# Input-projection tiles as eleven Strassen pairs in a stage of their own, with the gates of two heads beside the seventh pair

## The chip, the cores and the metric

The kernel runs on one core of one Trainium2 chip. The core has five engines with an instruction queue each: TensorE (PE, matrix products, with weight loads that overlap), VectorE (DVE), ScalarE (ACT), GpSimd (POOL) and SyncE (SP, which here only issues transfers). POOL issues transfers as well, and some of these add to what stands in their destination. The metric is the device time of one execution, in microseconds (us).

## The reference, cut to what matters

The kernel computes one decoder block for 512 tokens of width 1024, all in float32. The stage at issue is the first one, the normalised input times one wide weight matrix, and the gated linear attention (GLA) that uses a part of it:

```python
h = rms_norm(x, norm_mix_pre)                       # (512, 1024)
proj = h @ w_in                                     # split by columns:
g_q, g_k, g_v, g_r, g_a, n_q, n_kc, n_vc, n_ks, n_vs, n_kw, n_vw, n_gate, merge_gla, merge_nsa = split(proj)
# gla_mixer, 4 heads, keys of 128, values of 256, chunks of 64 tokens
log_a = log_sigmoid(g_a @ w_alpha2 + b_alpha) / 16
b = cumsum(log_a within a chunk)
qe, ke, kd = q * exp(b), k * exp(-b), k * exp(b_last - b)
o = causal(qe @ ke.T) @ v + qe @ state              # state: decayed sum of kd.T @ v over the chunks before
o = rms_norm(o, per head) * silu(g_r)
```

Behind it come a second attention (compressed, selected and window branches), a merge of the two, an output projection and a SwiGLU feed-forward network (FFN) of width 2816.

## The kernel before, in words

**Number format.** A float32 product is made of three matmuls: each operand is split into a high part (a cast by ACT, L70 or L211) and a low part, the difference to it (DVE, L76 or L212; or ACT writes the negated high part and a POOL transfer adds the raw values from memory to it, L74 and L1102). PE then adds high x high, high x low and low x high in one PSUM bank (`prod`, L194 to L196; the token stage, L274 to L276).

**Stages.** x arrives transposed in eight blocks of 128 features. *Token stage*: the columns whose result is wanted with tokens on the partitions (GLA values, the values of the other attention, its gates and the 16 columns of the low-rank gate) are made in three groups of 440 columns. *Feature-major tiles*: all other columns are made in tiles of 128 output features by 512 tokens, each 24 matmuls of 512 columns: per head a key tile (`gk`) and a query tile (`gq`), eight tiles `r` for the output gate, four query tiles and two key tiles for the other attention (`qst`, `kst`), four merge-gate tiles (`MA`). The weights of one tile (512 KB) are loaded by SP, one tile ahead, and split by the class `Stream`.

**GLA.** Each head has five steps: `gla_prep` (a scan of the log gates, exponentials on ACT, products with q and k on DVE and POOL), `gla_attn` (scores, mask, transposes of `ku`), `gla_state` (the state before each chunk pair), `gla_out` (output, its squares, the mean and its power on POOL, scaling on ACT) and `gla_end` (transposes, product with the output gate, split into `gla_hi` and `gla_lo`). Two more steps, `gates_low` and `gates_gla`, make the log gates of all four heads at once. `weave` spreads the steps of the heads over the tiles: while ACT, DVE and POOL work on a step, PE runs 24-matmul tiles. So the order of work on each engine is written out by the program; the engines take their queues strictly in order, and wait on semaphores.

**A form that exists already.** The FFN runs its gate and up projections as Strassen (Winograd) units: two tiles whose weights and input are cut into halves, seven products instead of eight (L1203), each 4 quarters x 3 = 12 matmuls of 256 columns, 84 for two tiles. Sums of the weights are made by DVE (L1133 to L1140) and split (L1118, L1125); the raw halves get their low part by an accumulating transfer (L1098 to L1102); DVE adds the products together (L1207) on top of a copy by ACT (L1220).

## Time and profile before

| | us |
|---|---|
| Time, median of 3 runs | 862.14 (861.67 to 862.71) |
| Profiled execution, its own time | 862.83 |
| Its span (first to last instruction) | 861.0 |
| PE busy | 846.4 (98%) |
| DVE busy | 596.1 (69%) |
| ACT busy | 485.9 (56%) |
| POOL busy | 142.9 (17%) |
| PE busy from 67 to 241 us (tiles with the GLA) | 173.9 of 174.0 |

In the groups of instructions a row reads: line, engine, operation, output <- input with shapes, count | busy us, mean ns of one | idle time of the engine just before, and what ended it. In a timeline and in the chain of waits the first number is the start in us from the span's start, the second its length; "x84" says that so many instructions stand in the row, and brackets give the idle time before it with its releaser. The chain of waits is the work that ended last, followed back from the end. Neighbouring matmuls overlap in the pipeline, so their price is the distance of their starts.

### The profile page before, as it was taken

How to read it: one execution, taken by the hardware profiler on the slowest of the kernel's cores; microseconds unless marked ns; L12 is line 12 of the kernel's file. 1: busy time of each engine (PE TensorE's matmuls, PEld its weight loads, DVE VectorE, ACT ScalarE, POOL GpSimd, SP SyncE). 2: the span in 40 equal slices, each digit the busy share in tenths (PEclk: the TensorE clock that was granted, in tenths of full speed). 3: DMA queues.
4: the chain of work that ended last, by engine and by line, in shares of the span. 5: the costliest groups of instructions: out<-in, count | busy, mean ns of one | idle time of the engine just before them, and what ended most of it. 6: DMA issues, size and time to landing. Idle time of an engine off the chain costs nothing.

```text
span 861.0 us, 13716 instructions
## 1 busy us (share of the span) xinstructions
PE 846.4 (98%) x5232; PEld 752.4 (87%) x5232; DVE 596.1 (69%) x1099; ACT 485.9 (56%) x866; POOL 142.9 (17%) x169
## 2 busy tenths in 40 slices
PE   8999999999999999999999999999999999999995
PEld 8998888888788788888887999899999999889995
DVE  7224763544466888887666478997778779829876
ACT  6335534333363888887634587666666557535441
POOL 1000322020030100010000265111211110001343
PEclk9999999999999999999999999999999999999998
DMA  6332222312241454445227759679787773325322
GB/s 230 107 95 99 81 93 70 90 57 79 93 144 61 102 120 120 102 106 115 64 84 260 231 152 246 130 181 234 172 180 196 193 164 77 96 89 172 87 99 99
DMA packets 37058, 111.23 MB, mean 129 GB/s; under 512 B 4252, under 2 KB 6572, under 8 KB 36864
## 3 DMA queue, kind: packets, MB, share of 16 engines
...
q14 instruction: 25, 0.20, 0.1%
...
## 4 chain that ended last, share of the span: by engine, by line
PE 91%; ACT 4%; DVE 2%; issue 1%; DMA 1%; POOL 0%; SPq 0%; ACTq 0%; POOLq 0%; DVEq 0%
PE ps_mm L194 11%; PE ps_mm L196 11%; PE ps_mm L195 11%; PE ps_mm L1203 6%; PE ps_tp L1203 6%; PE ps_sc L1203 6%; PE ps_acc L1203 5%; PE ps_sc L1494 4%; PE ps_acc L1494 2%; PE ps_mm L1494 2%; PE ps_tp L804 2%; PE ps_acc L194 1%; PE ps_acc L196 1%; PE ps_acc L195 1%; PE ps_sc L195 1%; PE ps_sc L194 1%
## 5 line engine op out<-in xcount | busy, mean ns | idle before, releaser
L70 ACT CAST whi<-wraw 128x1024 fp32r<-128x1024 f32 (+2 forms) x80 | 79.1, 989 | 149.9 <-PE ps_mm L195 69.5
L194 PE MATMUL ps_mm<-hT_hi,whi 128*128 128x512 f32 x344 | 139.7, 406 | 0.0
L196 PE MATMUL ps_mm<-hT_hi,wlo 128*128 128x512 f32 x344 | 136.8, 398 | 0.0
L195 PE MATMUL ps_mm<-hT_lo,whi 128*128 128x512 f32 x344 | 135.9, 395 | 0.0
L76 DVE TENSOR_TENSOR wlo<-wraw,whi 128x1024 fp32r<-128x1024 f32 (+2 forms) x65 | 74.9, 1152 | 50.9 <-ACT whi L70 50.9
L196 PEld LDWEIGHTS ps_mm<-hT_hi,wlo 128*128 128x128 f32 x344 | 64.6, 188 | 15.5 <-DVE wlo L76 0.3
L194 PEld LDWEIGHTS ps_mm<-hT_hi,whi 128*128 128x128 f32 x344 | 64.7, 188 | 14.1
L195 PEld LDWEIGHTS ps_mm<-hT_lo,whi 128*128 128x128 f32 x344 | 64.8, 188 | 13.1
L764 ACT ACTIVATE p<-p,mx 128x512 f32<-128x512 f32 (+1 forms) x64 | 35.9, 561 | 8.8 <-DVE mx L762 8.2
L212 DVE TENSOR_TENSOR pl<-ps_tp,ph 128x512 fp32r<-128x512 f32 (+1 forms) x64 | 31.0, 489 | 13.2 <-ACT ph L211 12.6
...
L762 DVE CUSTOM_DVE_ANT_0 p<-ps_sc,causal 128x512 f32<-128x512 f32 (+1 forms) x64 | 30.2, 486 | 6.1 <-PE ps_sc L755 6.0
L1102 POOL DMA_DIRECT2D w_uu<-in_w_up x19 | 16.4, 865 | 84.7 <-PE ps_sc L1203 27.1
L211 ACT CAST ph<-ps_tp 128x512 fp32r<-128x512 f32 (+1 forms) x64 | 26.4, 415 | 4.1 <-PE ps_tp L804 3.6
L804 PE MATMUL ps_tp<-ident,p 128*128 128x128 f32 x160 | 27.7, 273 | 0.4 <-ACT pc L698 0.3
L804 PEld LDWEIGHTS ps_tp<-ident,p 128*128 128x128 f32 x160 | 20.6, 140 | 8.0 <-ACT pc L698 0.7
L194 PE MATMUL ps_mm<-gla_hi,whi 128*128 128x512 f32 x64 | 26.2, 409 | 0.0
L196 PE MATMUL ps_mm<-gla_hi,wlo 128*128 128x512 f32 x64 | 25.2, 394 | 0.0
L195 PE MATMUL ps_mm<-gla_lo,whi 128*128 128x512 f32 x64 | 25.2, 394 | 0.0
L479 DVE TENSOR_TENSOR sr<-ps_mm,rb_x 128x512 f32<-128x512 f32 x8 | 5.5, 692 | 27.5 <-PE ps_mm L196 27.5
L1118 ACT CAST w_hl<-s 128x1024 fp32r<-128x1024 f32 x12 | 12.6, 1048 | 19.6 <-issue 15.8
L1118 ACT CAST w_d1h<-s 128x1024 fp32r<-128x1024 f32 x13 | 13.7, 1051 | 17.3 <-issue 12.6
...
## 6 DMA issues: line engine op xcount, KB each, us to landing
wraw<-in_w_t SPq DMA_DIRECT2D x40, 512.0 KB, 3.5
wraw<-in_w_gate SPq DMA_DIRECT2D x21, 512.0 KB, 5.7
rw<-in_w_up SPq DMA_DIRECT2D x19, 512.0 KB, 4.2
wlo<-wraw POOLq DMA_DIRECT2D x15, 512.0 KB, 4.6
wlo<-in_w_gate POOLq DMA_DIRECT2D x13, 512.0 KB, 6.9
w_uu<-in_w_up POOLq DMA_DIRECT2D x19, 256.0 KB, 5.8
...
wraw<-in_w_proj SPq DMA_DIRECT2D x8, 512.0 KB, 3.5
```

The source lines that it names most:

```text
L70: self.nc.scalar.copy(hi[:, :cols], raw[:, :cols])
L76: self.nc.vector.tensor_tensor(out=lo[:, :cols], in0=raw[:, :cols], in1=hi[:, :cols].bitcast(F32), op=OP.subtract)
L194: pe.matmul(ps[:, t], wh[:, c], xh(k)[:, t], start=(k == 0), stop=False)
L195: pe.matmul(ps[:, t], wh[:, c], xl(k)[:, t], start=False, stop=False)
L196: marks.append(pe.matmul(ps[:, t], wl[:, c], xh(k)[:, t], start=False, stop=(k == ktot - 1)))
L211: act.copy(hi, src)
L212: dve.tensor_tensor(out=lo, in0=src, in1=hi.bitcast(F32), op=OP.subtract)
L762: dve.tensor_tensor_reduce(out=o, in0=s, in1=causal[:, S - n:S], scale=-1.0, scalar=-NEG, op0=OP.add, op1=OP.min, accum_out=mx[:, i:i + 1])
L764: act.activation(out=o, in_=o, func=AF.Exp, scale=-1.0, bias=mx[:, i:i + 1], accum_out=z[:, i:i + 1])
L804: pe.transpose(tp[:, i * 128:(i + 1) * 128], p[:, OFF[i] + k * 128:OFF[i] + (k + 1) * 128], ident)
L1203: pe.matmul(o, w[:, c], x[q], start=(first and q == 0 and i == 0), stop=(q == 3 and i == 2), skip_group_check=True)
L1494: pe.matmul(o, w[:, c], x[q], start=(first and q == 0 and i == 0), stop=(q == KH - 1 and i == 2), skip_group_check=True)
```

## The change

22 of the feature-major tiles (four `gk` and `gq` pairs, eight `r`, `kst` s and w, four `qst`) leave the weave and become eleven Strassen pairs, run one after another in a stage of their own (`in_unit`; pairs are counted from 0 to 10). Each pair asks for 84 matmuls of 256 columns on PE, four sums and two lows on DVE, two sum casts and four raw-form instructions on ACT, and two accumulating transfers of 512 and 256 KB on POOL's queue. The input's sums (`t1` to `t4`) are made once, while the second token group runs. Of the three token groups the middle one ("B", the values of heads 1 to 3) moves behind the pairs. The log gates are made for two heads at a time: heads 0 and 1 inside the stage of the pairs, in the queues after pair 6 (the seventh), heads 2 and 3 in the GLA stage. The output gate is one `Silu` in place of `Tanh` and a product. In `gla_prep` two products move from POOL to DVE. The four heads are now woven with the 16 steps of token group B (six matmuls of 440 columns each) and the four `MA` tiles in 32 pieces of three matmuls, in the places that the table `when` gives. ACT loads its tables eight times up to the end of the GLA stage, where it was three times. The stages behind are as before.

Two places show the new order. The first is DVE's queue at the gates. Before (`lam` holds the log gates; `gk_588` and `gq_584` are tiles, `wlo` the low part of a weight tile):

```order
33 L364 TENSOR_SCALAR low<-ps_sc,vecs 128x512 x4
34 L310 TENSOR_TENSOR gk_588<-ps_mm,rb_x 128x512
35 L76 TENSOR_TENSOR wlo<-wraw,whi 128x1024
36 L370 TENSOR_TENSOR lam<-low,lam 128x512 x4
37 L376 SCALAR_TENSOR_TENSOR lam<-keep,lam 128x512
38 L312 SCALAR_TENSOR_TENSOR gq_584<-ps_mm,rb_x 128x512
39 L76 TENSOR_TENSOR wlo<-wraw,whi 128x1024
```

Now, beside pair 7 (L381 are the additions of products, `ps_tp` the banks of pair 7, `ps_sc` of pair 8; L336 to L339 the sums of weights, L206 a low part):

```order
153 L337 TENSOR_TENSOR ssum_165<-ssum_165,wraw 128x512
154 L206 TENSOR_TENSOR s1l<-ssum_166,s1h 128x1024
155 L433 TENSOR_TENSOR lam_1288<-ge_1293,lam_1288 128x512
156 L433 TENSOR_TENSOR lam_1288<-ge_1294,lam_1288 128x512
157 L434 SCALAR_TENSOR_TENSOR lam_1288<-ge_1290,lam_1288 128x512 x2
158 L381 TENSOR_TENSOR r_145<-ps_tp,us_493 128x256
159 L381 TENSOR_TENSOR r_144<-ps_tp,us_493 128x256
160 L402 TENSOR_TENSOR r_145<-r_145,rb_x 128x512
161 L381 TENSOR_TENSOR us_492<-ps_sc,us_492 128x256
```

The scans (L434) were between evacuations of plain tiles; now both stand directly ahead of two additions that empty banks which PE writes again within the same pair.

The second place is PE's queue at the first head's scores. Before:

```order
478 L194 MATMUL ps_mm<-hT_hi,whi 128x512
479 L195 MATMUL ps_mm<-hT_lo,whi 128x512
480 L196 MATMUL ps_mm<-hT_hi,wlo 128x512
481 L420 MATMUL ps_tp<-gq_888,gkx 128x128 x4
482 L427 MATMUL ps_tp<-ident,gku 128x128 x3
483 L194 MATMUL ps_mm<-hT_hi,whi 128x512
```

Now, in the GLA stage (L287 to L289 are the matmuls of token group B, of which 21 stand between the last product of pair 10 and the scores):

```order
1100 L289 MATMUL ps_acc<-wlo,hT_hi 128x440
1101 L287 MATMUL ps_acc<-whi,hT_hi 128x440
1102 L288 MATMUL ps_acc<-whi,hT_lo 128x440
1103 L289 MATMUL ps_acc<-wlo,hT_hi 128x440
1104 L594 MATMUL ps_tp<-gq_1806,gkx 128x128 x4
1105 L601 MATMUL ps_tp<-ident,gku 128x128 x3
1106 L287 MATMUL ps_acc<-whi,hT_hi 128x440
```

What the scores wait for (`gq`, `gkx`, `gku`) comes from `gla_prep(0)`. That step stood among plain tiles; now it begins on ACT after the last copy of pair 10, and the scores stand 21 matmuls behind that pair.

The diff, cut to its core:

```diff
-    with_gla = []
-    for h in range(HG):
-        with_gla += [("h", T_GK + h), ("h", T_GQ + h)]
...
+    for c in range(4):
+        st.plan(("B", c), I["w_tok"][1, :, c * 2 * TG:(c + 1) * 2 * TG], 2 * TG)
+    with_gla = [("h", T_MA + n) for n in range(4)]
...
+    pairs = [(T_GK + h, T_GQ + h) for h in range(HG)] + [(T_R + n, T_R + n + 1) for n in (0, 2, 4, 6)]
+    pairs += [(T_KV + 2, T_KV + 3), (T_NQ, T_NQ + 1), (T_NQ + 2, T_NQ + 3)]
+    NP = len(pairs)
...
+    def in_load(j):
+        g = wts.tile([128, 1024], F32, tag="wraw", bufs=3, name="wraw")
+        nc.sync.dma_start(g, I["w_t"][pairs[j][0]])
+        nc.sync.dma_start(urw[j % 2], I["w_t"][pairs[j][1]])
+        graw[j], uraw[j] = g, urw[j % 2]
+
+    def minus_high(hi, lo, raw, src):
+        act.copy(hi, raw)
+        act.activation(out=lo, in_=raw, func=AF.Copy, scale=-1.0)
+        return pool.dma_start(lo, src, accum_op=OP.add)
+
+    def in_raw_forms(j):
+        hi, lo = slot_of(j, "a")
+        minus_high(hi, lo, graw[j], I["w_t"][pairs[j][0]])
+        wf[j, "a11"], wf[j, "a12"] = [(hi[:, c], lo[:, c]) for c in (slice(0, 512), slice(512, 1024))]
+        t = uu[j % 2]
+        hi, lo = t[:, 0:512], t[:, 512:1024]
+        queued["pool"] = minus_high(hi, lo, uraw[j][:, 512:1024], I["w_t"][pairs[j][1], :, 512:1024])
+        wf[j, "a22"] = (hi, lo)
+
+    def in_sums(j):
+        g, u, (a, b) = graw[j], uraw[j], ssum
+        lo, hi = slice(0, 512), slice(512, 1024)
+        dve.tensor_tensor(out=a[:, lo], in0=u[:, lo], in1=u[:, hi], op=OP.add)
+        dve.tensor_tensor(out=a[:, hi], in0=a[:, lo], in1=g[:, lo], op=OP.subtract)
+        dve.tensor_tensor(out=b[:, lo], in0=g[:, lo], in1=u[:, lo], op=OP.subtract)
+        dve.tensor_tensor(out=b[:, hi], in0=g[:, hi], in1=a[:, hi], op=OP.subtract)
+
+    def slot_of(j, what):
+        n = 3 * j + (1 if what == "a" else 0 if what == "s1" else 2)
+        return slots[n % 5]
...
+    def in_unit(j):
+        tag = ("sc", "mm", "acc", "tp")[j % 4]
+        d1, d2 = [in_dst(n) for n in pairs[j]]
+        p1, p2 = bank(tag), bank(tag)
+        r1, rb, r2, ra = p1[:, 0:256], p1[:, 256:512], p2[:, 0:256], p2[:, 256:512]
+        us = us2[j % 2]
+
+        def product(o, a, b, first):
+            wh, wl = wf.pop((j, a))
+            for q in range(4):
+                c = slice(q * 128, (q + 1) * 128)
+                for i, (w, low) in enumerate(((wh, False), (wh, True), (wl, False))):
+                    pe.matmul(o, w[:, c], x_of(b, q, low), start=(first and q == 0 and i == 0),
+                              stop=(q == 3 and i == 2), skip_group_check=True)
+
+        def add(out, ps, b):
+            return dve.tensor_tensor(out=out, in0=ps, in1=b, op=OP.add)
+
+        product(r1, "a11", "b11", True)
+        act.copy(us[:, 0, :], r1)
+        product(r2, "s2", "t2", True)
+        add(us[:, 0, :], r2, us[:, 0, :])
+        product(rb, "s3", "t3", False)
+        add(us[:, 1, :], rb, us[:, 0, :])
+        product(ra, "s1", "t1", False)
+        add(d2[:, h1], ra, us[:, 1, :])
+        product(rb, "a22", "t4", False)
+        add(d2[:, h0], rb, us[:, 0, :])
+        product(ra, "s4", "b22", False)
+        add(d1[:, h1], ra, us[:, 0, :])
+        product(r1, "a12", "b21", False)
+        act.copy(d1[:, h0], r1)
+        for n, t in zip(pairs[j], (d1, d2)):
+            if T_NQ <= n < T_KV or n < T_GK:
+                queued["dve"] = dve.scalar_tensor_tensor(out=t, in0=t, scalar=0.125 if n >= T_NQ else QSCALE, in1=rb_x,
+                                                         op0=OP.mult, op1=OP.mult)
+            else:
+                queued["dve"] = dve.tensor_tensor(out=t, in0=t, in1=rb_x, op=OP.mult)
+            if n >= T_R:
+                act.activation(out=t, in_=t, func=AF.Silu)
+    def gate_logs(hs, lam, room, tag_low, tag):
+        w_a2, keep, aT, w3, *lows = room
+        pool.dma_start(w_a2, I["w_alpha2"])
+        pool.memset(keep, 1.0)
+        pool.memset(keep[:, :, 0:1], 0.0)
+        dve.memset(aT.bitcast(F32), 0.0)
+        dve.memset(w3.bitcast(F32), 0.0)
+        dve.tensor_copy(w3[0:16, :], w_a2)
+        dve.tensor_copy(w3[64:80, :], w_a2)
+        dve.tensor_tensor(out=w3[32:48, :], in0=w_a2, in1=w3[0:16, :].bitcast(F32), op=OP.subtract)
+        ps = bank(tag_low)
+        for i in range(NT):
+            pe.transpose(ps[0:16, i * 128:(i + 1) * 128], tokb[:, i, C_A:C_A + 16], ident)
+        act.copy(aT[0:16, :], ps[0:16, :])
+        act.copy(aT[32:48, :], ps[0:16, :])
+        dve.tensor_tensor(out=aT[64:80, :], in0=ps[0:16, :], in1=aT[0:16, :].bitcast(F32), op=OP.subtract)
+        for i, h in enumerate(hs):
+            ps = bank(tag)
+            pe.matmul(ps, w3[:, h * 128:(h + 1) * 128], aT, start=True, stop=True)
+            act.activation(out=lam[:, i], in_=ps, func=AF.Abs, bias=b_alpha[:, h:h + 1])
+            dve.tensor_scalar(out=lows[i], in0=ps, scalar1=b_alpha[:, h:h + 1], scalar2=0.0,
+                              op0=OP.add, op1=OP.min)
+        act.activation(out=lam, in_=lam, func=AF.Exp, scale=-1.0)
+        act.activation(out=lam, in_=lam, func=AF.Ln, bias=1.0)
+        for i, h in enumerate(hs):
+            dve.tensor_tensor(out=lam[:, i], in0=lows[i], in1=lam[:, i], op=OP.subtract)
+            dve.tensor_tensor_scan(out=lam[:, i], data0=keep.rearrange("p c t -> p (c t)"), data1=lam[:, i],
+                                   initial=0.0, op0=OP.mult, op1=OP.add)
+            lams[h] = lam[:, i]
...
+    def raw_sums():
+        for k in range(KD):
+            dve.tensor_scalar(out=X[:, k], in0=X[:, k], scalar1=g_pre[:, k:k + 1], scalar2=None, op0=OP.mult)
+        dve.tensor_tensor(out=t1, in0=b12, in1=b11, op=OP.subtract)
+        dve.tensor_tensor(out=t2, in0=b22, in1=t1, op=OP.subtract)
+        dve.tensor_tensor(out=t4, in0=b21, in1=t2, op=OP.subtract)
+        in_load(0)
+
+    def first_splits():
+        t_split("t2", t2)
+        t_split("t1", t1)
+        dve.tensor_tensor(out=b12, in0=b22, in1=b12, op=OP.subtract)
+        t_split("t3", b12)
+
+    def first_pair():
+        t_split("t4", t4)
+        in_load(1)
+        slots.append(sform0)
+        in_sums(0)
+        in_sum_forms(0, ("s1", "s2"))
+
+    side = [raw_sums, first_splits, first_pair, lambda: None]
...
+    for j in range(NP):
+        if j + 2 < NP:
+            in_load(j + 2)
+        if j == NP - 1:
+            st.ahead_to(1)
+        in_unit(j)
+        if j == 6:
+            with tc.issue_after(queued["dve"].ins), tc.issue_after(queued["pool"].ins):
+                early_gates()
+        if j + 1 < NP:
+            in_sums(j + 1)
+            in_sum_forms(j + 1, ("s1", "s2"))
+            in_sum_forms(j + 1, ("s3", "s4"))
+        if j + 2 < NP:
+            in_raw_forms(j + 2)
...
-        pool.tensor_tensor(out=q4[:, :, 2, :], in0=par(gq[h], 0), in1=e2[:, :, 0, :], op=OP.mult)
-        pool.tensor_tensor(out=kx[:, :, 1, :], in0=par(gk[h], 1), in1=e2[:, :, 1, :], op=OP.mult)
+        dve.tensor_tensor(out=q4[:, :, 2, :], in0=par(gq[h], 0), in1=e2[:, :, 0, :], op=OP.mult)
+        queued["dve"] = dve.tensor_tensor(out=kx[:, :, 1, :], in0=par(gk[h], 1), in1=e2[:, :, 1, :], op=OP.mult)
...
-            sr = srs.pop((h, f))
-            dve.scalar_tensor_tensor(out=sr, in0=ps, scalar=ghalf[:, f:f + 1], in1=sr, op0=OP.mult, op1=OP.mult)
-            split(ah[:, 2 * h + f, :], al[:, 2 * h + f, :], sr)
...
+            sr = gt.tile([128, S], F32, tag="sr", bufs=2, name="sr")
+            dve.scalar_tensor_tensor(out=sr, in0=ps, scalar=g_gla[:, f:f + 1], in1=rr[n], op0=OP.mult, op1=OP.mult)
+            ah[n] = mid.tile([128, S], F32R, tag="r%d" % n, name="gla_hi%d" % n)
+            split(ah[n], al[:, n, :], sr)
...
+    def values_step(c, i):
+        if (c, i) == (0, 0):
+            psb.extend(bank(t) for t in ("mm", "mm", "acc", "acc"))
+        if i == 0:
+            psb.append(st.next(("B", c)))
+        tok_chunk(psb[-1], psb, TG, c, (i,))
+        if c == 3:
+            scaled(tok01[:, i, TG:512], psb[i][:, 0:72], i)
+            scaled(tok23[:, i, 0:368], psb[i][:, 72:TG], i)
+            act.copy(tok23[:, i, 368:512], tokc[:, i, :])
+
+    fill = [lambda c=c, i=i: values_step(c, i) for c in range(4) for i in range(NT)]
+    q = Pieces(with_gla)
+    fill += [lambda: q.fill(1)] * (8 * len(with_gla))
+    when = {}
+    for at, f, h in ((0, gla_attn, 0), (0, gla_prep, 1), (4, gla_state, 0), (10, gla_attn, 1), (16, gla_out, 0),
+                     (16, gla_prep, 2), (17, gla_state, 1), (20, gla_end, 0), (21, gla_out, 1), (22, gla_prep, 3),
+                     (25, gla_end, 1), (27, gla_attn, 2), (29, gla_state, 2), (32, gla_out, 2), (33, gla_attn, 3),
+                     (36, gla_end, 2), (37, gla_state, 3), (40, gla_out, 3), (46, gla_end, 3)):
+        when.setdefault(at, []).append(lambda f=f, h=h: f(h))
+    gla_prep(0)
+
+    def gates23():
+        with tc.issue_after(queued["dve"].ins), tc.issue_after(queued["pool"].ins):
+            late_gates()
+
+    when[5] = [gates23]
```

More of the change, by code (lines that the diff above doesn't have):

```diff
@@ new lines, in hybrid_block_kernel, with squares @@
+    tfl = tf.tile([128, 4, 4, 256], F32R, name="tfl")
+    sform0 = [tf.tile([128, 1024], F32R, name="s0" + x) for x in "hl"]
+    acc_x = urw[1][:, 0:S]
+    sqs = [x[:, c] for x in ssum for c in (slice(0, S), slice(S, 2 * S))]
+    def squares(ks, after):
+        for k in ks:
+            sq = acc_x if k == 0 else sqs[k % 4]
+            with tc.issue_after(after.ins):
+                act.activation(out=sq, in_=X[:, k], func=AF.Square)
+            if k > 0:
+                dve.tensor_tensor(out=acc_x, in0=acc_x, in1=sq, op=OP.add)
@@ new lines, in hybrid_block_kernel @@
+    pss = [bank(t) for t in ("mm", "mm", "sc", "sc")]
+    for c in range(4):
+        w = tk.next(("tok", 0, c))
+        if c == 1:
+            squares(range(2, KD), tk.cast)
+        if c < 3:
+            tok_chunk(w, pss, TG, c)
+        else:
+            tok_chunk(w, pss, TG, c, range(0, 2))
+            ps = token_sums([acc_x], "acc")
+            rs_made = rsqrt_mean(rs_x, ps[:, 0:NT], D, EPS)
+            tok_chunk(w, pss, TG, c, range(2, NT))
+    x_rb = act.copy(rb_x, over_partitions(rs_x, "acc"))
@@ new lines, in first_splits @@
+    def first_splits():
[10 more added lines that the diff above has]
+    side = [raw_sums, first_splits, first_pair, lambda: None]
+    pss = [bank(t) for t in ("tp", "tp", "acc", "acc")]
+    for c in range(4):
+        tok_chunk(tk.next(("tok", 2, c)), pss, TG, c)
+        side[c]()
@@ new lines, in hybrid_block_kernel @@
+    for i in range(NT):
+        scaled(tokc[:, i, :], pss[i][:, 0:144], i)
+        scaled(tokb[:, i, :], pss[i][:, 144:TG], i)
+    p_in.__exit__(None, None, None)
+    p_s2 = tc.tile_pool(name="s2", bufs=1, reuse_waits="tile", side="right")
+    s2 = p_s2.__enter__()
+    slots += [[s2.tile([128, 1024], F32R, name="s%d%s" % (i, x)) for x in "hl"] for i in (1, 2)]
+    us2 = [s2.tile([128, 2, 256], F32, name="us%d" % i) for i in range(2)]
+    slots += [[wts.tile([128, 1024], F32R, tag="w" + x, bufs=2, name="w" + x) for x in ("hi", "lo")] for _ in range(2)]
@@ L355, in gates_gla @@
[L355 to L370 removed]
+    triu = param("triu", [128, 128], gt)
@@ L451, in gla_out @@
             out = ps[n // 2][:, (n % 2) * 256:(n % 2) * 256 + 256]
-            pe.matmul(out, at[:, n, :], tok[n][:, h * 256:(h + 1) * 256], start=True, stop=(n == 0))
+            pe.matmul(out, at[:, n, :], value(h, n), start=True, stop=(n == 0))
             if n > 0:
@@ L549, in hybrid_block_kernel @@
[L549 to L559 removed]
+    tok23 = gt.tile([128, NT, 512], F32, name="tok23")
```

300 lines of the change are left out of this document (133 added, 167 removed).

## The prediction, made before the changed kernel was run

> **What bounds the kernel now.** First the page's busy time by engine, then, from the list of what TensorE (PE) waited for, its first row and the one row of the token stage (columns: what waited, for what; us in total, times, the longest).
>
> ```profile
> PE 846.4 (98%) x5232; PEld 752.4 (87%) x5232; DVE 596.1 (69%) x1099; ACT 485.9 (56%) x866; POOL 142.9 (17%) x169
> PE ps_tp L232 <- POOL rs L226: 1.7, 2, 1.1
> ...
> PE ps_mm L276 <- DVE wlo L76: 0.9, 1, 0.9
> ```
>
> None of the list's other rows is above 1.1: PE waits for other engines about 6 us of 861.0. The table of stretches says whether the part that is changed has slack (columns: the stretch, its us, then busy us and instructions of PE, weight loads, DVE, ACT, POOL; last PEclk, DMA share, GB/s):
>
> ```profile
> 67.00:114.00 47.00, 47.00 (x209) 37.78 (x208) 30.50 (x38) 24.37 (x33) 8.14 (x8) 1.00 0.29 91
> 114.00:142.00 28.00, 28.00 (x127) 22.51 (x126) 14.30 (x20) 10.99 (x26) 6.84 (x7) 1.00 0.23 75
> 142.00:177.00 35.00, 34.98 (x163) 28.36 (x162) 16.44 (x24) 12.95 (x27) 6.11 (x7) 1.00 0.25 75
> 177.00:212.00 35.00, 34.97 (x163) 28.24 (x162) 16.16 (x22) 12.11 (x25) 5.07 (x5) 1.00 0.24 77
> 212.00:241.00 29.00, 28.97 (x135) 23.27 (x134) 12.11 (x18) 11.18 (x25) 3.69 (x6) 1.00 0.30 89
> ```
>
> PE is full from 67 to 241, at full clock. The kernel is PE-bound here, so a PE instruction saved is time saved. DVE and ACT are half idle, and every wait of the four GLA heads is hidden behind plain tiles. The change touches both sides of this: it takes away PE work, and with it the cover.
>
> **The PE work.** The chain of waits gives both prices. The first two rows are matmuls of 512 columns in the input projection, the others whole Strassen units of 84 matmuls of 256 columns in the FFN, a form that the change copies.
>
> ```profile
> 83.93 0.24 PE ps_mm L194
> ...
> 109.60 0.24 PE ps_mm L196
> ...
> 584.40 9.98 PE ps_tp L1203 x84
> ...
> 624.40 9.93 PE ps_tp L1203 x84
> ```
>
> From 83.93 to 109.60 lie 110 starts (every third is an L195, not shown among the longest): 25.67 / 110 = 0.233 us each, so a tile of 24 costs 5.60 and two cost 11.20. Four units in 624.40 - 584.40 = 40.00 make 10.00 each, 0.119 a matmul. The change makes eleven pairs: 11 x (11.20 - 10.00) = **-13.2 us**. It repeats the four gate transposes for the second half of the heads, at 0.11 each by the half width of a 256-column row: **+0.4**. All other matmuls stay.
>
> **The start.** In the chain the first 19 us read:
>
> ```profile
> 13.09 0.41 DVE w L344
> ...
> 15.04 0.42 DVE w L345
> ...
> 16.22 0.69 DVE w L346
> ...
> 17.62 0.99 DVE wlo L76
> 18.66 0.47 PE ps_mm L276
> 19.33 0.20 PE ps_mm L275
> ```
>
> Three gate preparations stand on DVE ahead of the low part (`wlo`) that the first token matmul waits for. They leave this place, 1.5 us by these rows, and the wait of 0.9 on L276 can go: **-0.9** (0 to -0.9, since two squares now share the place).
>
> **A pair's supply.** One FFN unit, and the groups that make up a unit's DVE and DMA work:
>
> ```profile
> 604.39:614.38 9.99, 9.99 (x87) 9.97 (x86) 7.97 (x15) 6.12 (x10) 1.73 (x2) 1.00 0.76 185
> ```
>
> ```profile
> L1125 DVE TENSOR_TENSOR w_hl<-s,w_hl 128x1024 fp32r<-128x1024 f32 x12 | 14.7, 1222 | 2.9 <-ACT w_hl L1118 2.9
> L1133 DVE TENSOR_TENSOR s<-rw 128x512 f32<-128x512 f32 x18 | 12.3, 686 | 0.1
> L1207 DVE TENSOR_TENSOR wk<-ps_sc,us 128x256 f32<-128x256 f32 x15 | 6.3, 421 | 3.0 <-PE ps_sc L1203 3.0
> wlo<-in_w_gate POOLq DMA_DIRECT2D x13, 512.0 KB, 6.9
> w_uu<-in_w_up POOLq DMA_DIRECT2D x19, 256.0 KB, 5.8
> ```
>
> A new pair asks of DVE four sums (2.7), two lows of the sums (2.4), five additions (2.1) and two multiplies by the norm (1.4 by the L1133 row): 8.6 of 10.0 us; the FFN unit runs with 8.0 and PE full. ACT has two sum casts, four raw forms and two copies, about 6 as there. The two accumulating transfers are issued when the fourth sum-product has freed its slot, about 8.5 us into the pair before last; with 6.9 to land, behind one issue, they are there near 17, and their first reader starts at 20. I cost all pairs but three at nothing: the work of the pair before hides them, and without that cover each would pay some 2 us. **First pair**: the forms of x are made during the second token group, 96 x 0.20 = 19.2 us of PE. Eight scalings of 512 columns, four sums and four lows of 1024 take DVE 8 x 0.69 + 8 x 1.22 = 15.3 at most, so it is done some 4 us ahead; 0, bounds 0 and 4 (the first accumulate late by its landing of 6.9 less the 3 of slack). **First output gate** (pair 5): a table load ahead of the next pair's copy, +0.5.
>
> **The gates beside the seventh pair.** ACT before, at the gates, and two DVE rows:
>
> ```profile
> 85.34 1.03 ACT L70 CAST whi<-wraw 128x1024 fp32r<-128x1024 f32 x1
> 86.40 1.28 ACT L368 ACT_TABLE_LOAD   x1
> 87.69 1.92 ACT L368 ACTIVATE lam<-lam 128x2048 f32<-128x2048 f32 x1
> ...
> 93.35 1.28 ACT L387 ACT_TABLE_LOAD   x1 [1.56 <-DVE lam L376]
> ...
> 96.07 0.64 ACT L392 ACTIVATE dd<-dd 128x512 f32<-128x512 f32 x1
> ```
>
> ```profile
> 89.64 2.50 DVE L370 TENSOR_TENSOR lam<-low,lam 128x512 f32<-128x512 f32 x4 [2.00 <-ACT lam L368]
> 92.06 1.22 DVE L376 TENSOR_TENSOR_SCAN lam<-keep,lam 128x512 f32<-128x512 f32 x1
> ```
>
> The two gate matmuls stand 30 rows into pair 7, 3.6 us. Behind them ACT does two `Abs` (512 columns each, like L392: 1.3), a load 1.3, an exponential of half L368's width 1.1, a cast of weights 1.0, a load 1.3, a logarithm 1.1: 7.1 us; then DVE two subtractions and two scans (1.25 + 2.45 = 3.7), and only then the addition of 0.4 that frees the bank of pair 7's last product: 3.6 + 7.1 + 3.7 + 0.4 = 14.8. That product stands 103 rows after the pair's first (some of pair 8 are ahead of it): 101 x 0.119 + 2 x 0.233 = 12.5. PE waits **+2.3**, and the rest of pair 8 with it. Bounds 0 (ACT gets ahead where it idled in the unit's 9.99) and 8 (all that the gates add to DVE: by the two rows and the L1133 row for two subtractions more, two half-wide memsets and the small casts, some 7.8).
>
> The Trainium skill (ScalarE: Activation LUTs, "What ACT_TABLE_LOAD costs") gives a switch 2.66 us, 1283 ns of load and some 1380 ns of drain. The trace shows the 1.28 and the next activation at 87.69, 1.29 after the load began, so I take 1.28; the page's price would add 2 x 1.4 to this wait.
>
> **The GLA stage.** Its cover is now 96 matmuls of 440 columns (0.20 each, 19.2) and 96 of 512 (22.4): 41.6 us. A head's own 39 instructions cost some 6 us (142 to 177: 163 instructions less 39 are 124 of 0.233, 28.9 of 35.0), so with the second gates the stage has about 68 us of PE work for four heads that had 28 to 35 each. The heads' waits surface at three places. *Start*: 21 matmuls of 440 and four of head 0 (4.7 us) stand ahead of the first transposes of `ku`. ACT needs a copy (0.4), a table load and the exponentials to `dd` (3.4 - 0.1 between 93.35 and 96.71 above): 3.7. Then POOL makes four products:
>
> ```profile
> 98.31 1.66 POOL L409 TENSOR_TENSOR gkx<-gk,dd 128x256 f32<-128x256 f32 x1
> 99.93 1.72 POOL L410 TENSOR_TENSOR gku<-gk,dd 128x256 f32<-128x256 f32 x1
> 101.60 1.06 POOL L411 TENSOR_TENSOR gku<-gkx,el 128x256 f32<-128x256 f32 x1
> ...
> 144.30 0.73 POOL L409 TENSOR_TENSOR gkx<-gk,dd 128x256 f32<-128x256 f32 x1
> 145.00 0.73 POOL L410 TENSOR_TENSOR gku<-gk,dd 128x256 f32<-128x256 f32 x1
> 145.69 0.62 POOL L411 TENSOR_TENSOR gku<-gkx,el 128x256 f32<-128x256 f32 x1
> 172.90 1.01 POOL L226 TENSOR_TENSOR grs<-grs,mhalf 128x4 f32<-128x4 f32 x1
> ```
>
> With a fourth at the price of L411's fast row they take 2.7 at the fast rows and 5.1 at the slow ones; middle 3.7. PE waits 3.7 + 3.7 - 4.7 = **+2.7** (1.7 to 4.1).
>
> The slow rows lie beside DVE's two-input work. The Trainium skill (Trainium Architecture — The Big Picture, "What this means for kernel authors") says that DVE and GpSimd share a port pair under an exclusive lock. The two speeds of L410 agree with it; taken whole, since DVE makes four products at the same time here, it gives the slow sum, 1.4 us more than mine.
>
> *Ends*: between a head's last output matmul and the transposes of its scaled rows lie a square, the POOL power and four ACT scalings:
>
> ```profile
> L460 ACT ACTIVATE go<-ps_acc,grs 128x256 f32<-128x256 f32 x16 | 6.3, 475 | 6.4 <-POOL grs L226 6.4
> L455 ACT ACTIVATE go<-ps_acc 128x256 f32<-128x256 f32 x16 | 6.1, 380 | 3.4 <-PE ps_acc L454 3.3
> ```
>
> 0.4 + 0.3 + 1.0 + four of 0.4 = 3.3 us; head 0 has nine matmuls of 0.233 (2.1) over it: +1.2. For head 1 about 0.7 more, since its mean stands on DVE behind head 0's output product and low: +1.9. Heads 2 and 3, +0.3 each, and 0.5 where the first outputs wait for ACT to empty the value banks. Stage together **+6.9** (bounds 1 and 14, when each chain is covered, or each head pays 3.3).
>
> **Sum**: -13.2 + 0.4 - 0.9 + 0.5 + 2.3 + 6.9 = -4.0 on the profiled execution's 862.8: 858.8; the median of the runs stands 0.7 lower (862.14), so **858.1 us**.
>
> **Rivals.** (a) *Waits hidden*: the 17 us of heads' matmuls and the pieces give way as the FFN does; the stage then pays 1.7, the gates 0.5: 858.1 - 5.2 - 1.8 = 851. For it: PE full for 174 us around the same chains before. Against: 68 us where there were 127 (114 to 241). (b) *The heads set the pace*, the slower side: place L601 and L642, where PE stands until ACT, DVE and POOL have finished a chain; from 11 us in the stage on it eats the gain. Price: both chains bare for every head, 2.7 + 3.3 = 6, times four is 24, of which the pieces cover a quarter to a half: 12 to 18, and 15 gives 866. For it: the transposes stand right behind the chains; against: ACT's queue is a third used in the table. (c) *DVE sets the pairs' pace*: 8.6 of 10.0, in order, and a copy or an addition late by 0.4 a pair: +4.4, 862.5, no change. Against: 8.0 in the FFN without a wait. (d) *Late accumulation*: slack 3 us; loads share the queues; 1 us in eight pairs gives 866. (e) *A switch costs twice its row*, by the rule above; two at the gates, one at the stage's start, one at the first output gate: 4 x 1.28 = 5.1, 863.2; the row at 87.69 speaks against it.
>
> **How the numbers follow.** Forecast 0.45 (own range 854 to 862), a 0.2, b 0.17, c 0.1, d 0.05, e 0.03. What can be told from no change is 0.2%, 1.7 us. Faster: 0.39 of the forecast, all of a, 0.03 of the rest: 0.62. Same: 0.05 + 0.08 (c, e) + 0.02 = 0.15. Slower: most of b and d, and c's upper part: 0.23. The range leaves out half of a below and a third of b above: 850 to 867.
>
> **What would show it.** Pairs 1 to 4 at 10.0 us a pair in the chain, or rival c or d with its releaser (DVE `us`, or the lows). One wait of about 2.3 on the bank of pair 7 with DVE as releaser. At the stage's start a wait on `gku` from POOL of 1.7 to 4.1, at L642 waits on ACT `go` of 1 to 2. No first wait on `wlo`. I am wrong if the stage's waits sum to over 11 us or under 3, or a pair takes over 10.4.

## The result, and the profile after

The changed kernel takes 868.41 us (median of 4 runs, 865.89 to 869.75) where the kernel before takes 862.19 (4 runs, 861.67 to 862.71): a ratio of 1.0064, 95% interval 1.0050 to 1.0077. It is slower by about 6 us; 858.1 was forecast, and 868.41 lies above the forecast's range of 850 to 867. The profiled execution took 869.75 us with a span of 868.0 (before 862.83 and 861.0). It is the slowest of the four, with a mean granted clock of 0.986; the other three have 0.990 to 0.992, so they lost less to a lowered clock than what is worked out below from the profile.

The page's busy times and its row of the granted clock (40 slices of the span):

```profile
PE 841.8 (97%) x5632; PEld 768.0 (88%) x5632; DVE 653.4 (75%) x1219; ACT 537.0 (62%) x953; POOL 154.9 (18%) x186
...
PEclk9999998999999999999999999999999999999997
```

PE is busy 4.6 us less than before (846.4), though the span is 7.0 longer, and the clock row has a dip in its seventh slice. What PE waited for now (columns: what waited, for what; us in total, times, longest):

```profile
PE ps_sc L377 <- DMA s0l<-in_w_t: 2.9, 1, 2.9
PE ps_sc L377 <- DMA s1l<-in_w_t: 2.2, 1, 2.2
...
PE ps_acc L626 <- ACT tok L292: 1.3, 1, 1.3
PE ps_tp L601 <- POOL gku L585: 1.3, 1, 1.3
PE ps_tp L642 <- ACT go L634: 1.1, 2, 0.7
...
PE ps_sc L377 <- ACT us L384: 0.6, 1, 0.6
PE ps_mm L188 <- ACT tok L292: 0.6, 1, 0.6
PE ps_sc L426 <- DVE gl L423: 0.5, 1, 0.5
PE ps_mm L377 <- ACT us L384: 0.5, 1, 0.5
PE ps_tp L594 <- DVE dec L569: 0.4, 1, 0.4
```

The two longest are accumulating transfers, of the first pair (`s1l`) and of pair 8 (`s0l`); the GLA stage has 5.2 in all (L626, L601, L642, L188, L426, L594). The chain of waits shows the pairs (start, length, engine or transfer, line, count):

```profile
38.68 9.88 DMA s1l<-in_w_t
48.61 11.55 PE ps_sc L377 x82
60.15 10.04 PE ps_mm L377 x84
70.19 9.97 PE ps_acc L377 x84
80.16 10.09 PE ps_tp L377 x84
...
122.42 9.00 DMA s0l<-in_w_t
```

Pairs 1 to 3 take 10.0 us as forecast; both transfers took 9 to 10 us, and **pair 0 takes 11.55 for 82 matmuls after its wait is over**. Why, the table of stretches tells. These stretches are 3.41 us long and are laid on the times at which the granted clock changes (columns: the stretch, its us, then busy us of PE, weight loads, DVE, ACT, POOL with their instructions; last PEclk, DMA share, GB/s):

```profile
45.10:48.51 3.41, 1.34 (x8) 1.06 (x6) 0.77 (x3) 3.37 (x8) 1.22 (x2) 1.00 1.03 323
48.51:51.92 3.41, 3.31 (x15) 3.32 (x16) 1.22 (x1) 0.37 (x1) 0.18 (x1) 0.50 1.04 277
51.92:55.34 3.42, 3.42 (x31) 3.42 (x30) 1.95 (x4) 0.00 (x0) 0.00 (x0) 1.00 0.91 259
127.02:130.43 3.41, 1.52 (x13) 1.31 (x11) 3.41 (x7) 3.38 (x4) 0.00 (x0) 1.00 1.06 261
130.43:133.85 3.42, 2.38 (x11) 2.38 (x12) 2.27 (x4) 2.55 (x3) 0.00 (x0) 0.50 0.14 54
133.85:137.26 3.41, 3.41 (x18) 3.41 (x18) 3.14 (x4) 0.91 (x2) 0.00 (x0) 0.50 0.00 0
137.26:140.67 3.41, 2.83 (x24) 2.62 (x24) 1.17 (x3) 2.66 (x5) 1.00 (x2) 1.00 0.37 49
195.29:198.70 3.41, 1.52 (x7) 0.68 (x5) 2.21 (x4) 3.41 (x12) 1.33 (x2) 1.00 0.31 68
198.70:202.11 3.41, 3.41 (x8) 2.76 (x9) 1.23 (x1) 1.91 (x5) 0.65 (x2) 0.50 0.44 106
```

Behind each of the three places where PE waited, the clock is at 0.50 for one or two whole stretches: 4 x 3.41 = 13.65 us, in which PE is busy for 12.5. PE's timeline shows the same matmul at both clocks, before and after the wait for `s0l` (start, length; in brackets the wait):

```profile
128.14 0.28 PE L377 MATMUL ps_tp<-tfl,s1h 128*128 128x256 f32 x1
128.25 0.28 PE L377 MATMUL ps_tp<-tfh,s1l 128*128 128x256 f32 x1
131.47 0.58 PE L377 MATMUL ps_sc<-hT_hi,s0l 128*128 128x256 f32 x1 [2.93 <-DMA s0l<-in_w_t]
131.85 0.41 PE L377 MATMUL ps_sc<-hT_hi,s0h 128*128 128x256 f32 x1
132.06 0.41 PE L377 MATMUL ps_sc<-hT_lo,s0h 128*128 128x256 f32 x1
```

The starts are 0.11 to 0.12 apart before and 0.21 after. So about half of the 12.5 busy us, an estimate of 6.3, went there. In the kernel before no stretch between 30 and 830 us is at half clock.

The first point that both kernels have in common behind the changed part is the compression of the second attention: 5.9 us later than before, so nearly all of the loss lies ahead of it.

```profile
258.17 2.06 PE L621 MATMUL ps_sc<-ct,cw 128*128 128x130 f32 x17
```

```profile
264.07 2.17 PE L804 MATMUL ps_sc<-ct,cw 128*128 128x130 f32 x18
```

### The profile page after: what moved, and what is told of

Same layout as the page of the kernel before. It is cut to its first block, busy times and chain, and to the rows that moved or that the text cites. A ratio compares the mean times of both kernels' runs of the same rounds, so it can differ in the third digit from the quotient of the medians.

```text
span 868.0 us, 14824 instructions
## 1 busy us (share of the span) xinstructions
PE 841.8 (97%) x5632; PEld 768.0 (88%) x5632; DVE 653.4 (75%) x1219; ACT 537.0 (62%) x953; POOL 154.9 (18%) x186
## 4 chain that ended last, share of the span: by engine, by line
PE 83%; ACT 6%; issue 3%; DMA 3%; DVE 2%; POOL 2%; SPq 0%; POOLq 0%; ACTq 0%; DVEq 0%
PE ps_mm L188 6%; PE ps_mm L190 6%; PE ps_mm L189 6%; PE ps_mm L1386 6%; PE ps_tp L1386 6%; PE ps_sc L1386 6%; PE ps_acc L1386 5%; PE ps_sc L1677 4%; PE ps_sc L377 3%; PE ps_mm L377 3%; PE ps_acc L377 2%; PE ps_mm L1677 2%; PE ps_acc L1677 2%; PE ps_tp L377 2%; PE ps_tp L987 2%
## 5 line engine op out<-in xcount | busy, mean ns | idle before, releaser
L70 ACT CAST whi<-wraw 128x1024 fp32r<-128x1024 f32 (+2 forms) x58 | 56.2, 969 | 53.7 <-issue 13.1
L188 PE MATMUL ps_mm<-hT_hi,whi 128*128 128x512 f32 x168 | 70.5, 420 | 0.6 <-ACT tok L292 0.6
L190 PE MATMUL ps_mm<-hT_hi,wlo 128*128 128x512 f32 x168 | 66.8, 398 | 0.0
L189 PE MATMUL ps_mm<-hT_lo,whi 128*128 128x512 f32 x168 | 66.8, 397 | 0.0
L76 DVE TENSOR_TENSOR wlo<-wraw,whi 128x1024 fp32r<-128x1024 f32 (+2 forms) x43 | 47.5, 1104 | 18.4 <-ACT whi L70 18.2
L206 DVE TENSOR_TENSOR pl<-ps_tp,ph 128x512 fp32r<-128x512 f32 (+1 forms) x64 | 31.0, 489 | 13.1 <-ACT ph L205 12.5
L190 PEld LDWEIGHTS ps_mm<-hT_hi,wlo 128*128 128x128 f32 x168 | 31.7, 189 | 7.7 <-DVE wlo L76 0.3
L188 PEld LDWEIGHTS ps_mm<-hT_hi,whi 128*128 128x128 f32 x168 | 31.8, 189 | 7.2 <-ACT tok L292 0.9
L189 PEld LDWEIGHTS ps_mm<-hT_lo,whi 128*128 128x128 f32 x168 | 31.9, 190 | 5.3
L188 PE MATMUL ps_mm<-gla_hi,whi 128*128 128x512 f32 x64 | 26.1, 408 | 0.0
L322 POOL DMA_DIRECT2D uu<-in_w_t x11 | 9.7, 883 | 84.8 <-ACT uu L321 78.0
L1301 ACT CAST w_d1h<-s 128x1024 fp32r<-128x1024 f32 x13 | 13.7, 1051 | 17.2 <-issue 12.5
```

The lines of the kernel that those rows point to most:

```text
L70: self.cast = self.nc.scalar.copy(hi[:, :cols], raw[:, :cols])
L76: self.nc.vector.tensor_tensor(out=lo[:, :cols], in0=raw[:, :cols], in1=hi[:, :cols].bitcast(F32), op=OP.subtract)
L188: pe.matmul(ps[:, t], wh[:, c], xh(k)[:, t], start=(k == 0), stop=False)
L189: pe.matmul(ps[:, t], wh[:, c], xl(k)[:, t], start=False, stop=False)
L190: marks.append(pe.matmul(ps[:, t], wl[:, c], xh(k)[:, t], start=False, stop=(k == ktot - 1)))
L206: dve.tensor_tensor(out=lo, in0=src, in1=hi.bitcast(F32), op=OP.subtract)
```

## The experiments

All ratios are to the kernel before on the same chip, with a 95% interval. The theory was that a wait costs its length and, where it is long, a stretch of half clock too; the first rival was that waits cost their length alone, later ones are named with their runs.

**1. The two late transfers.** *First pair alone*: its low part by DVE instead of a transfer.

```diff
-        minus_high(hi, lo, graw[j], I["w_t"][pairs[j][0]])
+        if j == 0:
+            split(hi, lo, graw[j])
+        else:
+            minus_high(hi, lo, graw[j], I["w_t"][pairs[j][0]])
```

> Edit: the low part of pair 0's first raw tile (a11, a12) is made by a DVE subtraction (1.22 us) in place of the accumulating transfer that landed 9.9 us after its issue. Theory, waits and clock: PE's wait of 2.2 us in front of pair 0 goes, and with it the stretch of 3.4 us at half clock that follows it, 1.7 us more: 868.4 - 3.9 = 864.5, and no clock below 1.0 between 48 and 60 us. Rival, a wait costs its own length alone (the half clock has another cause, the load of the transfers or the dense 256-column matmuls): 866.2, with the half clock still there.

864.86 us, 1.0016 [1.0007, 1.0026]: some 4 us of the 6 come back, more than the wait of 2.2. The wait for `s1l` is gone, a shorter one on ACT's copy (1.7) took its place, and a half-clock stretch behind it is still there; the wait for `s0l` is as long as in the changed kernel, but **no** half clock followed it in this execution.

```profile
PE ps_sc L380 <- DMA s0l<-in_w_t: 2.8, 1, 2.8
PE ps_sc L380 <- ACT us L387: 2.3, 2, 1.7
```

That fits neither theory as it stood: a wait of 2.8 left the clock alone, one of 1.7 did not. The 864.5 that was expected was met, but partly by luck: the half clock between 48 and 60 us, which was to go, stayed, and the two stretches of it behind `s0l`, which the edit doesn't touch, are missing.

*Pairs 7 and 8 in order*: pair 8's first two products bound behind pair 7's last (in the changed kernel some 26 matmuls of pair 8 stand inside pair 7).

```diff
+        with tc.issue_after(queued["pe"].ins) if j in (8,) else nullcontext():
+            product(r1, "a11", "b11", True)
```

> Edit: the matmuls of pair 8 are kept behind the last one of pair 7 on PE (in the changed kernel 26 of them were put ahead). Theory, the early reader: the 2.9 us wait for the accumulated low part of pair 8 goes, since its reader starts some 8 us later; but PE then meets the bank that DVE empties only after the two scans, 14.8 us after pair 7's start where PE is there after 10.5: a wait of about 4 us takes its place, with a half clock behind it: 868 to 869. Rival, the scans delay nothing that PE needs: the 2.9 us, the 0.6 behind and the 3.4 lost to two windows of half clock all go: 861.5.

870.54 us, 1.0075 [1.0058, 1.0091]: nothing gained. The wait for `s0l` is gone, so it was there only because its reader stood early; in its place PE waits for what the gates hold up on ACT and DVE:

```profile
PE ps_mm L377 <- ACT whi L320: 2.8, 1, 2.8
...
PE ps_tp L377 <- DVE r L381: 1.1, 1, 1.1
```

The second row is the wait that the prediction had named (the addition behind the scans). *In order, and the scans behind pair 7's additions*:

```diff
+        if j == 7:
+            with tc.issue_after(queued["dve"].ins):
+                scan_logs(*later_work.pop())
```

> Edit: as the run with the pairs in order, and the two subtractions and two scans of the early gates are queued on DVE behind pair 7's last multiply. Theory, scans and early reader together: both waits go, 2.9 + 0.6 + 3.4 = 6.9 less at most 1 us given back in pair 8, which now has the scans beside it: 862 to 862.5, and a granted clock of 1.0 between 121 and 150 us. Rival, wait alone without clock: 865.

865.92 us, 1.0032 [1.0023, 1.0042]: 2.8 us of the loss come back, where 6 were expected. Both waits went and the clock is full between 121 and 150 us, but a new wait of 1.9 on ACT's copy (`us`) stands in their place. *Both repairs*, the edits of the first and of this run together:

> Edit: the low part of pair 0 on DVE, the pairs in order, the scans behind pair 7. Theory, waits and clock: 3.9 + 6.4 less than the changed kernel: 858, which is faster than the kernel before; one half-clock window is left, in the stage of the heads. Rival, waits alone: 862.7.

863.85 us over ten executions, of which one took 2899.8 us (863.49 over the other nine), 1.0009 [0.9995, 1.0023]: no difference to the kernel before. The 858 of the theory was missed: two waits on ACT's copies (2.9 together) came up, and the GLA stage's waits and its half-clock stretch are still there. Eleven pairs that save some 11 to 13 us of PE are worth nothing yet.

**2. Which wait halves the clock.** The kernel before, with waits of graded length in eight FFN units:

```diff
+        if n in PROBE:          # {5: 1, 7: 4, 9: 7, 11: 10, 13: 13, 15: 16, 17: 6, 19: 9}
+            for i in range(PROBE[n]):
+                act.copy(scr, ra[:, 0:96])
+            held["pe"] = pe.transpose(r2[0:96, 0:128], scr[:, 0:96], ident).ins
```

> The kernel before, with artificial waits of TensorE in eight FFN units: behind the product S4 ScalarE copies 96 columns 1, 4, 7, 10, 13, 16, 6 and 9 times, and TensorE transposes the copy before it goes on. By the copies of 128x256 (0.35 us, about 0.25 apart) each copy is some 0.25 us, so that the waits should run from about 0.5 to about 4 us, together some 17 us. Theory 'the clock follows the waits': the units with waits of about 2 us and more are followed by a stretch of 3.4 us at half clock, those with waits under about 1.5 are not; each such stretch costs 1.7 us more than the wait itself. Rival 'the halves in the changed kernel came from the transfers or from dense work': the granted clock stays at 1.00 behind every wait, and each unit is longer by its wait alone.

905.17 us, 1.0486 [1.0465, 1.0507]. The waits came out longer than meant (28.2 us together) and the span is 43.5 longer: 15 us are not wait. They are the clock: eleven stretches are at half clock, PE is busy for 29.5 us in them, and half of that is 14.7. PE's timeline at the first four, and the stretches around the second and the fourth:

```profile
574.39 0.31 PE L1245 MATMUL ps_mm<-ident,probe 128*96 128x128 f32 x1 [1.16 <-ACT probe L1243]
...
596.91 0.31 PE L1245 MATMUL ps_tp<-ident,probe 128*96 128x128 f32 x1 [2.32 <-ACT probe L1243]
...
621.66 0.45 PE L1245 MATMUL ps_mm<-ident,probe 128*96 128x128 f32 x1 [3.14 <-ACT probe L1243]
...
647.13 0.45 PE L1245 MATMUL ps_tp<-ident,probe 128*96 128x128 f32 x1 [3.95 <-ACT probe L1243]
```

```profile
594.08:597.49 3.41, 1.09 (x10) 0.89 (x9) 3.41 (x7) 2.49 (x7) 0.86 (x1) 1.00 0.54 77
597.49:600.91 3.42, 3.42 (x18) 3.42 (x18) 1.42 (x3) 1.63 (x3) 0.00 (x0) 0.50 1.04 321
...
641.87:645.28 3.41, 1.32 (x12) 1.11 (x10) 3.41 (x6) 3.12 (x8) 0.86 (x1) 1.00 0.57 71
645.28:648.69 3.41, 1.56 (x8) 1.56 (x9) 1.92 (x4) 1.61 (x7) 0.00 (x0) 0.50 0.91 251
648.69:652.11 3.42, 3.42 (x18) 3.42 (x18) 0.43 (x1) 2.14 (x3) 0.00 (x0) 0.50 0.27 109
```

Behind 1.16 the clock stays at 1.00; behind 2.32, 2.86 and 3.14 it is at 0.50 for one stretch, behind 3.95, 4.46, 4.76 and 5.58 for two. So the rival falls, and so does the one that transfers or dense work halve the clock: the waits here are on ACT, and without them the same units ran at full clock. The price of one stretch: the unit of 2.32 and the one behind it take 13.35 + 10.68 where two take 20.00, so 4.0 for a wait of 2.3, which is its length and half a stretch of 3.41.

**3. Is the transfer slow, or does it share?** The changed kernel, with the loads of pairs 2 and 3 held until the first pair's transfer has landed:

```diff
+        if j in (2, 3):
+            for t in (g, urw[j % 2]):
+                pool.tensor_copy(t[:, 0:1], slot_of(0, "a")[1][:, 0:1].bitcast(F32))
         nc.sync.dma_start(g, I["w_t"][pairs[j][0]])
```

> The changed kernel, with the loads of pairs 2 and 3 (four of 512 KB) held on their queue until the accumulating transfer of the first pair's raw form has landed: a column of each target is written from the landed low part first. In the profile after, that transfer landed in 9.9 us with all 16 DMA engines busy (share 1.01, 269 GB/s from 38 to 49 us). Theory 'it is late by what it shares the engines with': it lands in 6 to 7 us as the fastest of the others do (6.0), TensorE's wait of 2.2 to 2.9 goes, and the half-clock stretch behind it: about 3 to 4 us less, 864.5. Rival 'an accumulating transfer of this size takes 9 to 10 us there': wait and time stay as they are, 868.

864.33 us, 1.0009 [0.9994, 1.0023]: 4.7 us of the 6 come back (by the ratios) by holding four loads. The transfer lands in 7.9 instead of 9.9 us (chain of waits), and PE waits 0.2 for it instead of 2.2:

```profile
39.35 7.91 DMA s1l<-in_w_t
```

So two of the 9.9 us come from the transfers beside it: in this run four loads that overlapped it, and one more accumulating transfer, start behind it, and the DMA share over its flight is 0.71 where it was 1.00. The rest isn't explained: 6 to 7 were expected.

**4. The GLA stage.** On top of both repairs the heads' pieces stand two to four places later in the table `when`:

```diff
-    for at, f, h in ((0, gla_attn, 0), (0, gla_prep, 1), (4, gla_state, 0), (10, gla_attn, 1), (16, gla_out, 0),
+    for at, f, h in ((2, gla_attn, 0), (0, gla_prep, 1), (6, gla_state, 0), (11, gla_attn, 1), (19, gla_out, 0),
...
```

> The repairs of both places (first pair's low part on VectorE, gates' scans behind the seventh pair) and the heads' pieces two to four places later in the row of the GLA stage. Theory 'the stage's waits are a matter of place': of the stage's 5.2 us of waits about 1.5 are left, and its half-clock stretch (1.7 us) goes: about 858.5 where the repairs alone had 863.9. Rival 'the heads set the stage's pace': the waits come back at other rows, in sum 4 to 6 us, and the time stays at 862 to 865.

861.95 us, 0.9990 [0.9978, 1.0002]: 1.6 less (by the ratios) than with the repairs alone, not 5. The half-clock stretch went, but the waits moved to other rows. Then ACT was cleared ahead of two copies as well (results of the token group emptied behind the first pair's first copy, two `Silu` behind the eighth pair's):

```diff
+        if j == 0:
+            with tc.issue_after(queued["us"].ins):
+                tok_out()
...
+        if j == 8:
+            silu_after_copy()
```

> As the run before, and two more edits on ScalarE: the second token group's results are emptied behind the first copy of the first pair, and the two Silu of the seventh pair stand behind the first copy of the eighth. Theory 'a wait costs its length, and half a window of clock where it is long': the waits of 0.9 (first pair) and 2.0 (eighth pair) on the copy go: 2.9 less than the run before, about 855.5. Rival 'ScalarE is short of time there': the copies are late by other work in its queue, and the time is that of the run before within 1.

859.48 us, 0.9961 [0.9947, 0.9975]: both waits on the copy are gone, 2.5 us by the ratios where 2.9 were expected. Next, pieces bound behind rows of PE instead of places in the table (head 0's transposes behind the sixth step of the value tile, head 1's end behind two more pieces, the late gates three steps later):

```diff
+    def behind_tok(h):
+        with tc.issue_after(queued["tok"].ins):
+            gla_attn(h)
...
-    for at, f, h in ((2, gla_attn, 0), (0, gla_prep, 1), (6, gla_state, 0), (11, gla_attn, 1), (19, gla_out, 0),
+    for at, f, h in ((0, gla_prep, 1), (5, behind_tok, 0), (9, gla_state, 0), (12, gla_attn, 1), (19, gla_out, 0),
...
-                     (30, gla_end, 1), (30, gla_attn, 2), (32, gla_state, 2), (35, gla_out, 2), (36, gla_attn, 3),
+                     (30, gla_attn, 2), (32, behind_piece, 1), (32, gla_state, 2), (35, gla_out, 2), (36, gla_attn, 3),
...
-    when[5] = [gates23]
+    when[8] = [gates23]
```

> The fastest of the runs so far (859.5: both repairs, heads' pieces later, ScalarE cleared), and three pieces bound behind rows of TensorE: head 0's transposes behind the sixth step of the value tile, the late gates three steps later, head 1's end behind two more pieces of a merge tile. Theory 'each wait left is a matter of place': of the waits on gku (1.3), gkx (0.4), gl (0.9), gs (0.6) and go (1.3) about 1 us is left: about 856. Rival 'the chain of a head is as long as the cover': they come back at the next row of the same chain, and the time is 859 to 860.

860.84 us, 0.9975 [0.9966, 0.9985]: the waits on `gku`, `gkx` and `go` are gone, and one of 3.0 is new, with two stretches at half clock behind it; one bad place ate what three good ones gave.

```profile
PE ps_sc L447 <- DVE gl L444: 3.0, 1, 3.0
```

DVE waited 3.5 us there for the gates' small weights, whose transfer POOL issues behind two heads' products. So the late gates were cut in three (weights and constants ahead of the first head, casts at step 6, matmuls behind step 11), once on the changed kernel alone and once with all repairs:

```diff
+    late = gate_steps((2, 3), lam23, gate_room(lambda shape, dt, i: gt.tile(shape, dt, tag="late%d" % i, name="gl%d" % i)),
+                      "tp", "sc")
+    next(late)
...
-    when[8] = [gates23]
+    when[6] = when.get(6, []) + [gates23]
+    when[11] = when.get(11, []) + [gates23_rest]
```

> The changed kernel with only the GLA stage put otherwise: heads' pieces later, head 0's transposes behind the sixth step of the value tile, head 1's end behind two more pieces of a merge tile, and the late gates in three parts: weights and constants on GpSimd ahead of the first head, small casts at step 6, the matmuls behind step 11. The first pair and the seventh stay as the change has them. Theory 'three places, each its waits and its windows of clock': the stage's waits of 5.2 us fall to about 1 and its half window (1.7 us) goes: about 6 less than 868.4, 862.5. Rival 'the heads set the stage's pace': 867 to 869.

863.59 us, 1.0004 [0.9991, 1.0016]: the GLA stage put otherwise gives 5 of the 6 us back by itself. This run settles what experiment 1 left open. Its profile has the waits for `s1l` (1.7) and `s0l` (2.9) of the changed kernel, and one of 2.3 on `gs`, and its clock is at full from 6 to 848 us:

```profile
46.43:49.85 3.42, 1.75 (x15) 1.54 (x14) 1.06 (x1) 2.33 (x5) 0.87 (x1) 1.00 1.06 316
49.85:53.26 3.41, 3.41 (x31) 3.41 (x30) 1.73 (x5) 0.37 (x1) 0.00 (x0) 1.00 1.03 308
124.93:128.34 3.41, 1.85 (x16) 1.65 (x14) 3.41 (x7) 3.38 (x5) 0.00 (x0) 1.00 1.05 262
128.34:131.75 3.41, 2.10 (x17) 2.10 (x18) 2.26 (x3) 2.88 (x3) 0.00 (x0) 1.00 0.23 90
131.75:135.17 3.42, 3.42 (x32) 3.42 (x31) 3.42 (x6) 2.50 (x4) 0.86 (x1) 1.00 0.00 0
```

The wait of 2.9 is cut by the border of two stretches into 1.56 and 1.31, and neither half is enough. This execution was the fastest of its ten (860.76; the slowest, 866.41, had a mean clock of 0.988 instead of 0.994).

With the repairs of the first and the seventh pair and the two edits on ACT beside it:

> The repairs of all three places: first pair's low part on VectorE, the gates' scans behind the seventh pair, ScalarE cleared ahead of the copies, and the GLA stage put as in the run beside it. The wait of 3.0 on the late gates' low part, behind which the granted clock halved for 6.8 us in the run before, should go, and with it 3.0 + 3.4 of 860.8: about 854.5. By the prediction's sum with every wait at nothing: -13.2 + 0.4 - 0.9 = 13.7 less than 862.1, 848.5, with some 4 us of short waits left in the pairs 852.5. Rival 'what one wait gives back another takes': 859 to 861.

859.49 us, 0.9954 [0.9937, 0.9971]: 854.5 was missed, the rival holds. A wait of 2.3 on head 1's state copy, behind head 2's exponentials on ACT, had taken the place of the one removed, again with a stretch at half clock. That copy was put ahead of the exponentials:

```diff
-                     (16, gla_prep, 2), (18, gla_state, 1), (24, gla_end, 0), (25, gla_out, 1), (22, gla_prep, 3),
+                     (16, gla_state, 1), (17, behind_state, 2), (24, gla_end, 0), (25, gla_out, 1), (22, gla_prep, 3),
...
```

(`behind_state` queues head 2's `gla_prep` behind the copy of head 1's first state.)

> The run with all places repaired (859.5), and head 1's state copy ahead of head 2's exponentials on ScalarE, where TensorE had waited 2.3 us for it with a half-clock stretch of 3.4 us behind. Theory by the traces so far, 'a stretch at half clock follows a window of the clock's 3.41 us grid in which TensorE idles more than about 1.7 us, whatever it waits for': with this wait gone none is left that can fill such a window ahead of the FFN; 2.3 + 1.7 less, about 855.5, runs within 1 us of one another, and no record at half clock before the last 15 us. Rival 'what one wait gives back another takes': 858.5 to 860.

**855.95 us, 0.9906 [0.9891, 0.9921]**, five runs from 854.13 to 856.40: faster than both kernels. The time is the one expected, and no record is at half clock between 7 and 845 us; only the spread of the runs, 2.3 us, is more than the 1 that was named. PE's waits in the part that was changed are now these and some of 0.5 to 0.7:

```profile
PE ps_sc L654 <- ACT gs L656: 1.2, 1, 1.2
...
PE ps_sc L384 <- DVE us L388: 0.7, 2, 0.4
```

The page's clock row can't show this: one half-clock stretch in a slice of 21.4 us still leaves a 9. Over 100 us it shows (columns as in the table of stretches; this run twice, then the run before it):

```profile
30.00:130.00 100.00, 97.91 (x758) 95.26 (x757) 83.15 (x129) 68.68 (x99) 16.34 (x20) 1.00 0.73 176
130.00:230.00 100.00, 97.64 (x593) 86.97 (x592) 69.64 (x113) 61.59 (x132) 23.45 (x30) 1.00 0.30 78
```

```profile
130.00:230.00 100.00, 95.69 (x576) 84.62 (x576) 68.12 (x109) 59.65 (x125) 24.11 (x29) 0.98 0.28 73
```

## Why the prediction was wrong, point by point

To the common point (258.17 before, 264.07 after) the sum was -4.0, and +5.9 was measured:

| term | predicted | measured in the profile after |
|---|---|---|
| eleven pairs | -13.2 | -12.9 (pairs 1 to 3: 10.03 each) |
| gate transposes | +0.4 | not told apart (taken as +0.4) |
| start | -0.9 | -1.7 (first pair at 46.04, the row that followed the token groups before at 47.74) |
| first pair's wait | 0 | +2.2 |
| first output gate | +0.5 | +0.5 |
| gates beside the seventh pair | +2.3 | +3.8 (2.9, 0.6, 0.3) |
| GLA stage's waits | +6.9 | +5.2 |
| half clock (estimate) | not in the sum | +6.3 |
| not assigned | | +2.1 |

The pairs were sized well, and the stage's waits well enough. **The step that failed is the one that runs through all terms: a wait was priced at its own length.** The kernel before never waits long enough ahead of the FFN's end to show what a wait does to the clock, and the sum had no term for it; in the profiled execution 6.3 of the 9.9 us of error are this. Without it that execution would be at 863.4, beside 862.83 before: no difference. The rest of the error is smaller and is spread over the first pair, the gates and the PE work, as follows.

*First pair*: 0 was chosen from bounds 0 and 4, though the slack of 3 us was worked out with a landing of 6.9 from the FFN. At that place five of SP's loads overlap its flight (DMA share 1.03 in the first stretch above), and it landed in 9.9. Experiment 3 shows that the transfers beside it did 2.0 of these 3 us.

*Gates beside the seventh pair*: the size was near, the mechanism not. The bank behind the scans was to be waited for; the first wait was for pair 8's transfer, because the order puts that pair's matmuls into pair 7. The working counted these matmuls as PE's cover and didn't ask whether their weights had landed; its "first reader starts at 20" doesn't hold for a reader that stands a pair early. Only with the pairs in order (experiment 1) did the predicted wait show, at 1.1, beside 2.8 on ACT that the working had not followed: the weights' casts stand in ACT's queue behind the gates.

*GLA stage*: start 1.7 (the lower bound, though POOL's four products took 3.4 us, 172.48 to 175.90: near the middle of 3.7 and not the slow sum of 5.1, with DVE's products beside them), ends 1.1 against 3.7, and 1.9 on the emptying of the value banks where 0.5 was put.

*Rivals*. The heads set the pace (b) gave 866, close to the result, but not by its mechanism: the stage holds 5.2 of waits and one half-clock stretch, not 15, and the GLA stage's new places alone (experiment 4) took most of it away. Waits hidden (a) is what the last run approaches, after all the edits of experiments 1 and 4. DVE sets the pairs' pace (c) falls: 10.0 a pair. Late accumulation (d) was real in two pairs, not eight. A switch at twice its row (e) has nothing for it in the profile after: each load took 1.28 and the next activation began 1.29 after the load did.

*Not assigned*. The last run misses 1.6 in the same way, since its common point comes 8.2 ahead of before (249.94), where -12.9 + 0.4 - 1.7 and its waits of 4.4 would make 9.8. Most of both is PE work that the sum had no term for. Taken from start to start, with waits and lost clock left out, PE's work from the start of the part (47.74 before, 46.04 after, 45.90 in the last run) to the common point is 210.4 us before, 199.6 after and 199.7 in the last run: 10.8 less, and not the 12.5 of the table's first two rows. "All other matmuls stay" holds for their number but not for their price: in the last run the 168 matmuls of the plain tiles that are left of the part take 0.249 us each where 696 took 0.238 before, and the 96 of the value group 0.207 where they took 0.200. Why they take longer in the new order isn't shown.
